# Six of eight u/gate pairs five tile pairs wide, eleven halves of their block sums by adding DMAs, every second pair with u first

## The chip, the cores and the metric

The kernel runs on one core of one Trainium2 chip. The metric is device time in microseconds for one execution. A core has a matrix engine (TensorE, PE in the profile, with its weight loads as PEld), a vector engine (VectorE, DVE), an activation engine (ScalarE, ACT), GpSimd (POOL) and a queue processor (SyncE, SP). DMAs are issued from the queues of SP, ACT and POOL and are carried out by the core's 16 DMA engines.

## The reference

Two decoder layers over a sequence of 256 rows with 2048 columns, then a norm. Only the first projection of the first layer matters here: `a_w_in` has 2048 rows and 3 x 4096 columns, u, v and gate.

```python
def gmlp_branch(xn, w_in, v_g, w_s, b_s, w_out):
    proj = xn @ w_in
    uv = jax.nn.gelu(proj[..., :2 * GMLP_WIDTH])
    zg = proj[..., 2 * GMLP_WIDTH:]
    u, v = jnp.split(uv, 2, axis=-1)
    v = rms_norm(v, v_g)
    ...
    mixed = jnp.einsum('gts,bnsgc->bntgc', ws, vc) + ...
    y = u * mixed * jax.nn.silu(zg)
    return y @ w_out
```

xn is 256 x 2048 here, w_in 2048 x 12288, and all data are float32.

## The kernel before, in words

**Products.** Every large product is a left side of 256 rows (two tiles of 128, t = 0 and 1) with a weight matrix. The weights come in k tiles of 128 rows and column blocks of 512. A tile is cut into a rounded high part (`cut`, line 114, on ACT) and the rest (line 115, on DVE), so that three matmuls (`terms`, lines 119 to 121: high by high, high by low, low by high) give a product of float32 accuracy. `cut` takes two tiles at a time, [128, 2, 512], or one, [128, 1, 512]; its results live in `wspl`, which has five buffers for each part.

**Pairs.** A `Pair` computes two column blocks j = 0 and 1 at once. For KS of its k tile pairs (one tile from each list of `HALVES`) it uses a scheme of seven block products instead of eight: with the left side's blocks a11 to a22 and the weights' blocks b11 (first list, column 0), b12 (first list, column 1), b21, b22 (second list), the products are called p1 to p7. The left side's sums S1 to S4 are made once (`Left.sums`, `Left.fifth`, `sums_of`). The weights' sums are made in place in b11 and b12. In the order of the code:

- `head`: p1 with b11 as it was loaded (bank a); then b11 becomes b12 - b11 (`minus`, line 286, DVE), and b12 gets b22 added (`plus`, line 294: a DMA issued by GpSimd that reads b22 from memory again and adds it); p5 with the new b11 (bank e); then b22 is added to b11 (line 314 on DVE for the first two groups, a DMA for the fifth tile).
- `body`: p6 with that b11 (bank b, begun from a copy of a); p2 with b21 (bank a); p7 with b12 (bank c, begun from a copy of b); then b11 becomes b21 - b11 (line 339, `minus`, DVE); p3 with b22 (bank b); p4 with the last b11 (bank d, begun from a copy of c).
- `column(0)` and `column(1)`: the k tiles outside the scheme, `rest`, two at a time, for both row tiles t; each step is 12 matmuls. Then `evac` takes the finished banks. `column(1)` of one pair runs in steps between the blocks of the next pair's head and body (`run`).

With 16 k tiles a pair has 7 x KS + 4 x (16 - 2 KS) = 64 - KS tile products of three matmuls.

**Groups and buffers.** `groups` cuts the KS tiles of a block into halves of two tiles and, when KS is 5, a fifth tile alone. With `fifth_first` the fifth comes first in p1 and p5 (`early`). Each half of b11, b12, b21 and b22 has one buffer in `sraw`, the fifth tiles of b11 and b12 have one each in `ex`, and the fifth tiles of b21 and b22 (`others`) and the tiles of `rest` share the three buffers of `wraw`.

**The stages.** v (columns of v, KS 4); gu (this case: eight pairs b = 0 to 7, column 0 the gate block, column 1 the u block, KS from `KS_GU`); o (the output product of the first layer); qk, bv and bg (the second layer); f (its output product). In gu, `mid_gu` between body and `column(0)` runs `mixing` for the pair: GpSimd loads `ws` behind the last adding DMA (line 596) and masks it (line 601), ACT and DVE cut it (lines 603 and 604), six matmuls mix (lines 616 to 618), ACT adds the bias (line 620). `evac_gu` applies silu to column 0 and gelu to column 1 on ACT (line 625) and multiplies y by it on DVE (at once for column 0, line 627; from a queue for column 1, line 532). When ACT goes from one of the two functions to the other it loads a table first (ACT_TABLE_LOAD at line 625).

**Order of work.** Each engine and each queue runs its own instructions in order. That order is fixed when the kernel is built, by a planner that simulates the engines' times and takes the work that is ready, mainly in the order of the code.

## Time and profile before

| | |
|---|---|
| median of 3 runs (lowest, highest) | 1143.83 us (1143.17, 1144.0) |
| profiled execution | 1143.73 us |
| its span, first to last instruction | 1142.0 us |
| mean granted TensorE clock | 0.998 |
| DMA packets | 264.72 MB, mean 232 GB/s |
| of it by GpSimd's queue (q0) | 33.04 MB, 15.7% of the 16 engines' span |
| of it by SP's queue (q1) | 227.57 MB, 56.9% |

How to read the lines: a row of groups gives source line, engine, operation, output<-inputs by the program's names, their shapes and the count, then the busy time in us and the mean ns of one, then the idle time of the engine just before them and what ended it. `gu_b` are the tiles of b11 to b22, `gu_p_hi` and `gu_p_lo` their cut parts, `gu_raw`, `gu_hi` and `gu_lo` the same for the columns, and `gu_a` to `gu_e` the banks (`gu_b` on TensorE is bank b). A row of windows gives the busy time of each engine in a stretch of the span, the granted clock, the DMA engines' mean busy share and GB/s. A row of the timeline gives start, length, engine, line and operation; neighbours of one kind are merged with a count.

### The profile page before, as it was taken

To read this page: it belongs to the slowest core of one execution; us is meant where nothing else is said; L and a number is where in the kernel's file an instruction comes from. 1 tells how busy PE (TensorE), PEld (TensorE's weight loads), DVE (VectorE), ACT (ScalarE), POOL (GpSimd) and SP (SyncE) were. 2 spreads that over 40 slices of the span, in tenths; PEclk is the share of its full clock that TensorE was granted. 3 is DMA by queue.
4 is the path that set the end of the run, shared out by engine and by line. 5 is a ranking of instruction groups with operands and counts; after the bars stand their busy time and mean duration, and the time that the engine had idled before them with its cause. 6 is when DMAs were issued, how large, how long until landed. Compare 5 with 4: busy or idle time off the path is not lost.

```text
span 1142.0 us, 14838 instructions
## 1 busy us (share of the span) xinstructions
PE 1132.6 (99%) x5168; PEld 939.5 (82%) x5168; DVE 1011.7 (89%) x1111; ACT 830.6 (73%) x1102; POOL 88.7 (8%) x106
## 2 busy tenths in 40 slices
PE   9999999999999999999999999999999999999997
PEld 6888888888888888888888888888888888888886
DVE  7989899988998999978988788989889989897986
ACT  8776777777787778866657456788678887886564
POOL 0300110100110110000010001100100101000000
PEclk9999999999999999999999999999999999999999
DMA  9978687686687786685785877687687766837962
GB/s 343 333 270 275 206 257 265 199 262 243 183 269 254 186 264 241 175 289 142 266 258 166 294 211 266 159 266 210 179 287 193 215 234 174 265 90 241 343 213 87
DMA packets 79083, 264.72 MB, mean 232 GB/s; under 512 B 8992, under 2 KB 9504, under 8 KB 78880
## 3 DMA queue, kind: packets, MB, share of 16 engines
q1 hardware_dynamic: 67040, 227.57, 56.9%
q0 software_dynamic: 10672, 33.04, 15.7%
q10 hardware_dynamic: 1296, 3.17, 0.7%
q8 instruction: 40, 0.66, 0.2%
q14 instruction: 35, 0.29, 0.1%
HBM read 259.55 MB, written 4.19 MB: 231 GB/s over the span
## 4 chain that ended last, share of the span: by engine, by line
PE 98%; ACT 0%; DMA 0%; issue 0%; SPq 0%; POOLq 0%; POOL 0%; DVE 0%; ACTq 0%
PE gu_a L121 3%; PE gu_a L120 3%; PE gu_b L121 3%; PE gu_b L120 3%; PE gu_a L119 3%; PE gu_b L119 3%; PE op_acc L119 2%; PE op_acc L121 2%; PE op_acc L120 2%; PE gu_d L121 2%; PE gu_c L121 2%; PE gu_d L119 2%; PE gu_d L120 2%; PE gu_c L120 2%; PE gu_c L119 2%; PE v_acc L120 1%
## 5 line engine op out<-in xcount | busy, mean ns | idle before, releaser
L114 ACT CAST gu_p_hi<-gu_b 128x1024 fp32r<-128x1024 f32 (+1 forms) x126 | 123.2, 1004 | 37.5 <-PE gu_c L121 17.5
L115 DVE TENSOR_TENSOR gu_p_lo<-gu_b,gu_p_hi 128x1024 fp32r<-128x1024 f32 (+1 forms) x126 | 143.1, 1166 | 2.9 <-ACT gu_p_hi L114 2.4
L115 DVE TENSOR_TENSOR qk_p_lo<-qk_b,qk_p_hi 128x1024 fp32r<-128x1024 f32 (+1 forms) x77 | 80.8, 1075 | 10.6 <-ACT qk_p_hi L114 10.1
L114 ACT CAST qk_p_hi<-qk_b 128x1024 fp32r<-128x1024 f32 (+1 forms) x77 | 70.5, 934 | 25.1 <-PE o_c L121 6.3
L115 DVE TENSOR_TENSOR gu_lo<-gu_raw,gu_hi 128x1024 fp32r<-128x1024 f32 x60 | 72.1, 1220 | 7.6 <-ACT gu_hi L114 7.3
L114 ACT CAST gu_hi<-gu_raw 128x1024 fp32r<-128x1024 f32 x60 | 61.9, 1052 | 18.9 <-DMA gu_raw<-in_a_w_in 7.9
L115 DVE TENSOR_TENSOR v_lo<-v_raw,v_hi 128x1024 fp32r<-128x1024 f32 (+1 forms) x41 | 48.9, 1195 | 13.5 <-ACT v_hi L114 13.4
L114 ACT CAST v_hi<-v_raw 128x1024 fp32r<-128x1024 f32 (+1 forms) x41 | 41.7, 1027 | 25.7 <-DMA v_raw<-in_a_w_in 20.2
L115 DVE TENSOR_TENSOR v_p_lo<-v_b,v_p_hi 128x1024 fp32r<-128x1024 f32 x42 | 50.4, 1221 | 4.8 <-ACT v_p_hi L114 4.6
L114 ACT CAST v_p_hi<-v_b 128x1024 fp32r<-128x1024 f32 x42 | 43.2, 1049 | 9.5 <-PE v_c L121 5.7
L115 DVE TENSOR_TENSOR bg_p_lo<-bg_b,bg_p_hi 128x1024 fp32r<-128x1024 f32 (+1 forms) x42 | 42.5, 1042 | 5.3 <-ACT bg_p_hi L114 5.3
L114 ACT CAST o_p_hi<-o_b 128x1024 fp32r<-128x1024 f32 (+1 forms) x35 | 33.4, 965 | 18.4 <-PE op_acc L121 13.4
L115 DVE TENSOR_TENSOR bv_p_lo<-bv_b,bv_p_hi 128x1024 fp32r<-128x1024 f32 (+1 forms) x42 | 42.5, 1041 | 4.4 <-ACT bv_p_hi L114 4.2
L114 ACT CAST bv_p_hi<-bv_b 128x1024 fp32r<-128x1024 f32 (+1 forms) x42 | 37.4, 907 | 10.0 <-PE qk_c L121 4.0
L114 ACT CAST bg_p_hi<-bg_b 128x1024 fp32r<-128x1024 f32 (+1 forms) x42 | 37.2, 907 | 8.9 <-PE bg_a L121 2.5
L115 DVE TENSOR_TENSOR o_p_lo<-o_b,o_p_hi 128x1024 fp32r<-128x1024 f32 (+1 forms) x35 | 38.3, 1113 | 5.4 <-ACT o_p_hi L114 5.4
L286 DVE TENSOR_TENSOR gu_b<-gu_b,gu_b 128x1024 f32<-128x1024 f32 (+1 forms) x36 | 41.3, 1164 | 0.1
L114 ACT CAST op_hi<-op_raw 128x1024 fp32r<-128x1024 f32 x24 | 25.0, 1052 | 19.0 <-PE op_acc L121 9.1
L114 ACT CAST o_hi<-o_raw 128x1024 fp32r<-128x1024 f32 x22 | 23.0, 1054 | 21.2 <-DMA o_raw<-in_a_w_out 12.1
L120 PE MATMUL op_acc<-op_lo,yc 128*128 128x512 f32 x96 | 37.8, 394 | 0.0
L115 DVE TENSOR_TENSOR o_lo<-o_raw,o_hi 128x1024 fp32r<-128x1024 f32 x22 | 26.7, 1224 | 12.3 <-ACT o_hi L114 12.0
L121 PE MATMUL op_acc<-op_hi,yc 128*128 128x512 f32 x96 | 37.6, 393 | 0.0
(798 smaller groups left out, 3775.8 us busy)
## 6 DMA issues: line engine op xcount, KB each, us to landing
gu_b<-in_a_w_in SPq DMA_DIRECT2D x64, 512.0 KB, 4.7
gu_raw<-in_a_w_in SPq DMA_DIRECT2D x60, 512.0 KB, 5.2
v_raw<-in_a_w_in SPq DMA_DIRECT2D x32, 512.0 KB, 5.2
qk_b<-in_b_w_in SPq DMA_DIRECT2D x32, 512.0 KB, 4.8
qk_raw<-in_b_w_in SPq DMA_DIRECT2D x26, 512.0 KB, 5.4
v_b<-in_a_w_in SPq DMA_DIRECT2D x24, 512.0 KB, 4.9
op_raw<-in_a_w_out SPq DMA_DIRECT2D x24, 512.0 KB, 4.5
o_raw<-in_a_w_out SPq DMA_DIRECT2D x22, 512.0 KB, 4.3
```

Source lines behind the costliest of these rows:

```text
L114: nc.scalar.copy(hi[:, sl], raw[:, sl])
L115: low[0] = nc.vector.tensor_sub(lo[:, sl], raw[:, sl], f(hi[:, sl]))
L119: nc.tensor.matmul(acc, lh, hi, start=first, stop=False, skip_group_check=True)
L120: nc.tensor.matmul(acc, lh, lo, start=False, stop=False, skip_group_check=True)
L121: nc.tensor.matmul(acc, ll, hi, start=False, stop=last, skip_group_check=True)
L286: nc.vector.tensor_sub(into[g], b0[g], b1[g])
```

## The change

Three settings change, and with them the signs of the sums.

- `KS_GU` goes from (4, 4, 4, 5, 4, 5, 4, 4) to (4, 5, 5, 5, 5, 5, 5, 4): pairs 1, 2, 4 and 6 become five tile pairs wide.
- A new list `FAR_GU` says for each pair how many of b11's two halves get b21 by an adding DMA, issued in the code right behind p6, in place of the DVE instruction ahead of p3: 0, 2, 2, 1, 2, 1, 2, 1, eleven halves in all. The fifth tile's sum stays on DVE.
- In every pair of odd number u is column 0 and the gate column 1, so that gelu ends one pair and begins the next, and then silu does.
- For a sum that a DMA can make, b21 must be added: so in the first two groups b11 is kept with its sign reversed (b11 - b12, then minus b22), S1 of the fifth tile and S2 of the others change sign to match, and the copy of bank e to `es` gets a scale of -1. This holds for the pairs of all stages.

```diff
-KS_GU = (4, 4, 4, 5, 4, 5, 4, 4)
+KS_GU = (4, 5, 5, 5, 5, 5, 5, 4)
+FAR_GU = (0, 2, 2, 1, 2, 1, 2, 1)
...
-        def minus(self, into, b0, b1, order=None):
-            for g in order or range(len(self.groups)):
-                nc.vector.tensor_sub(into[g], b0[g], b1[g])
-
-        def plus(self, into, i, j, g0=0):
+        def plus(self, into, i, j, g0=0, g1=9):
             for g in self.early:
-                if g < g0:
+                if not g0 <= g < g1:
                     continue
                 k, n = self.groups[g]
                 adds.append(nc.gpsimd.dma_start(into[g], self.src(HALVES[i][k], n, j), accum_op=ALU.add))
...
-            self.minus(self.b11, self.b12, self.b11, self.early)
+            for g in self.early:
+                b = (self.b11[g], self.b12[g])[::1 if g < 2 else -1]
+                nc.vector.tensor_sub(self.b11[g], *b)
...
             for g in range(len(self.b22)):
-                nc.vector.tensor_add(self.b11[g], self.b22[g], self.b11[g])
+                nc.vector.tensor_sub(self.b11[g], self.b11[g], self.b22[g])
...
-            nc.scalar.copy(es, e)
+            nc.scalar.activation(es, e, AF.Identity, scale=-1.0)
             block(b11, lambda k: left.sum_part(1, k), b, "p6")
+            self.plus(b11, 1, 0, 0, self.far)
...
-            self.minus(b11, b21, b11)
+            for g in range(self.far, len(self.groups)):
+                (nc.vector.tensor_add if g < 2 else nc.vector.tensor_sub)(b11[g], b21[g], b11[g])
...
-            nc.scalar.activation(sg, bank, (AF.Silu, AF.Gelu_apprx_tanh)[j], scale=r1[:, t:t + 1])
+            nc.scalar.activation(sg, bank, (AF.Silu, AF.Gelu_apprx_tanh)[(j + b) % 2], scale=r1[:, t:t + 1])
...
-            run(Pair(columns(a_w_in, 2 * W + b * CB, b * CB), left, KD, f"gu{b}", KS_GU[b],
-                     lambda j, t, bank, b=b: evac_gu(b, j, t, bank), mid=lambda pair, b=b: mid_gu(b, pair), fifth_first=True))
+            cs = 2 * W + b * CB, b * CB
+            run(Pair(columns(a_w_in, *cs[::-1 if b % 2 else 1]), left, KD, f"gu{b}", KS_GU[b],
+                     lambda j, t, bank, b=b: evac_gu(b, j, t, bank), mid=lambda pair, b=b: mid_gu(b, pair), fifth_first=True,
+                     far=FAR_GU[b]))
```

More of the change, by code (lines that the diff above doesn't have):

```diff
@@ L149, in sums @@
                 nc.vector.tensor_sub(s3, a21, a11)
-                nc.vector.tensor_sub(s2, a11, s1)
-                nc.vector.tensor_sub(s4, a12, s2)
+                nc.vector.tensor_sub(s2, s1, a11)
+                nc.vector.tensor_add(s4, a12, s2)
                 for i, si in enumerate((s1, s2, s3, s4)):
@@ L166, in fifth @@
             a11, a12, a21, a22 = full[:, 0, 0:P], full[:, 1, 0:P], full[:, 0, P:S], full[:, 1, P:S]
-            nc.vector.tensor_sub(sm[:, 0], a21, a22)
-            nc.vector.tensor_sub(sm[:, 1], a11, sm[:, 0])
+            nc.vector.tensor_sub(sm[:, 0], a22, a21)
+            nc.vector.tensor_add(sm[:, 1], a11, sm[:, 0])
             nc.vector.tensor_sub(sm[:, 2], a21, a11)
@@ L185, in sums_of @@
             nc.vector.tensor_sub(s13, a21, a22)
-            nc.vector.tensor_sub(s24, a11, s13)
+            nc.vector.tensor_sub(s24, s13, a11)
             split(0, s13)
@@ L189, in sums_of @@
             nc.vector.tensor_sub(s13, a21, a11)
-            nc.vector.tensor_sub(s24, a12, s24)
+            nc.vector.tensor_add(s24, a12, s24)
             split(2, s13)
@@ L233, in trunk_kernel, with __init__ @@
     class Pair:
-        def __init__(self, src, left, nk, name, ks, evac, mid=None, fifth=None, fifth_first=False):
+        def __init__(self, src, left, nk, name, ks, evac, mid=None, fifth=None, fifth_first=False,
+                     far=0):
             self.fifth = fifth or (lambda j, name: ex.tile([P, 1, CB], F32, tag=f"b1{j + 1}_2", name=name))
             self.src, self.left, self.name, self.ks = src, left, name, ks
-            self.evac, self.mid = evac, mid
+            self.evac, self.mid, self.far = evac, mid, far
             self.rest = [k for k in range(nk) if k not in HALVES[0][:ks] + HALVES[1][:ks]]
@@ L623, in evac_gu @@
             y = v_of(t, b * CB, CB)
-            sg = jk.tile([P, CB], F32, tag=f"sg{t}", bufs=1, name=f"{'gu'[j]}{b}_{t}")
-            nc.scalar.activation(sg, bank, (AF.Silu, AF.Gelu_apprx_tanh)[j], scale=r1[:, t:t + 1])
+            sg = jk.tile([P, CB], F32, tag=f"sg{t}", bufs=1, name=f"{'gu'[(j + b) % 2]}{b}_{t}")
+            nc.scalar.activation(sg, bank, (AF.Silu, AF.Gelu_apprx_tanh)[(j + b) % 2], scale=r1[:, t:t + 1])
             if j == 0:
```

## The prediction

> **What bounds the kernel now.** I read the chain of work that ended last first, then the stage that the change touches.
>
> ```profile
> PE 98%; ACT 0%; DMA 0%; issue 0%; SPq 0%; POOLq 0%; POOL 0%; DVE 0%; ACTq 0%
> ```
>
> The chain is TensorE almost from end to end: time is saved by giving it less to do, and lost where something else is late. The gu stage is the eight u/gate pairs. Below are the busy times from the mixing matmuls of pair 0 to those of pair 7, seven pair periods, with the first period alone above them, and one TensorE group of that window.
>
> ```profile
> core 0: us, PE busy (x) PEld busy (x) DVE busy (x) ACT busy (x) POOL busy (x), PEclk, DMA share, GB/s
> 194.61:236.77 42.16, 42.16 (x187) 34.92 (x186) 41.08 (x42) 31.98 (x37) 3.29 (x4) 1.00 0.75 233
> 194.61:488.50 293.89, 293.89 (x1300) 243.47 (x1299) 274.02 (x279) 226.51 (x270) 28.54 (x32) 1.00 0.74 230
> ```
>
> ```profile
> L121 PE MATMUL gu_a<-gu_p_hi,x_lo 128*128 128x512 f32 x60 | 23.4, 389 | 0.0
> ```
>
> TensorE is busy for all of the window, at clock 1.00, with 0.0 us of idle time before its instructions. A pair of width four has 3 x (7 x 4 + 4 x 8) = 180 matmuls and 6 for the mixing; 42.16 / 186 = 0.2267 us is what one matmul occupies (its mean of 389 ns is the pipelined duration). VectorE (DVE) is busy for 274.02 of 293.89 us, 93%, ScalarE (ACT) 77%, the DMA engines 74%: DVE is next in line.
>
> **Part 1, width five.** In general a pair has 3 x (64 - KS) matmuls. Pairs 1, 2, 4 and 6 go from four to five, 3 fewer each: 12 x 0.2267 = 2.72 us off TensorE. All of it is on the path if the others still deliver.
>
> What the others do for it, by the groups of the same window (DVE, then ACT):
>
> ```profile
> L115 DVE TENSOR_TENSOR gu_p_lo<-gu_b,gu_p_hi 128x1024 fp32r<-128x1024 f32 x98 | 117.8, 1225 | 2.5 <-ACT gu_p_hi L114 2.1
> L115 DVE TENSOR_TENSOR gu_lo<-gu_raw,gu_hi 128x1024 fp32r<-128x1024 f32 x54 | 64.9, 1219 | 3.2 <-ACT gu_hi L114 3.0
> L286 DVE TENSOR_TENSOR gu_b<-gu_b,gu_b 128x1024 f32<-128x1024 f32 x28 | 33.8, 1225 | 0.1
> ...
> L115 DVE TENSOR_TENSOR gu_p_lo<-gu_b,gu_p_hi 128x512 fp32r<-128x512 f32 x14 | 9.6, 683 | 0.0
> ...
> L286 DVE TENSOR_TENSOR gu_b<-gu_b,gu_b 128x512 f32<-128x512 f32 x4 | 2.7, 682 | 0.0
> ...
> L574 DVE TENSOR_TENSOR yc<-yT,yc 128x512 fp32r<-128x512 f32 x1 | 0.7, 690 | 0.2 <-ACT yc L573 0.2
> ```
>
> ```profile
> L114 ACT CAST gu_hi<-gu_raw 128x1024 fp32r<-128x1024 f32 x52 | 53.7, 1052 | 13.3 <-PE gu_d L121 6.6 <-DMA gu_raw<-in_a_w_in 2.3 <-DVE gu_lo L115 2.2
> L625 ACT ACT_TABLE_LOAD x14 | 18.0, 1283 | 0.2
> ...
> L114 ACT CAST gu_p_hi<-gu_b 128x512 fp32r<-128x512 f32 x14 | 8.7, 620 | 2.5 <-DMA gu_b<-in_a_w_in 0.8 <-PE gu_c L121 0.6 <-PE gu_b L121 0.5
> ...
> L328 ACT COPY gu_es<-gu_e 128x512 f32<-128x512 f32 x7 | 4.1, 588 | 2.1 <-PE gu_e L121 2.0
> ```
>
> A wider pair cuts seven half tiles more (one per block) and two full ones less (one per column), and makes two half sums more, for its first and third block sums. DVE: 4 x (7 x 0.683 - 2 x 1.219 + 2 x 0.682) = +14.8 us. ACT: 4 x (7 x 0.620 - 2 x 1.052) = +8.9 us.
>
> **Part 2, eleven sums by DMA.** Eleven of the L286 subtractions leave DVE: 11 x 1.225 = -13.5 us. DVE's fourteen groups (the first and the last are shown above) add to 288.8 us for 279 instructions where its busy time is 274.0, so each overlaps its neighbour by 0.05 us; the 17 instructions more in parts 1 and 2 give 0.9 back. Net for DVE +0.4 us: 274.4 of the new 291.2 us, 94% where it was 93%. On average it keeps up; where it is dense is rival B.
>
> In their place stand 11 adding DMAs on GpSimd's queue, and the wider pairs add two half-size ones each:
>
> ```profile
> L294 POOL DMA_DIRECT2D gu_b<-in_a_w_in x18 | 15.7, 870 | 207.3 <-DVE gu_b L286 137.7 <-DMA gu_raw<-in_a_w_in 55.1 <-ACT g L625 9.5
> L601 POOL TENSOR_SCALAR_AFFINE_SELECT ws<-ws 128x256 f32<-128x256 f32 x7 | 8.9, 1269 | 46.1 <-DMA ws<-in_wst 46.1
> ```
>
> ```profile
> q0 software_dynamic: 2928, 9.31, 17.5%
> ...
> gu_b<-in_a_w_in SPq DMA_DIRECT2D x8, 256.0 KB, 5.8
> ws<-in_wst POOLq DMA_DIRECT2D x7, 128.0 KB, 7.5
> ```
>
> ```profile
> DMA to landing us min/median/max: 4.1/6.9/8.6
> ```
>
> (The last row is GpSimd's adds.) Issue: 19 x 0.870 = 16.5 us on an engine busy for a tenth of the window. Does an add arrive in time? It has to wait until its half of b11 has been cut for p6, and p4's cut waits for it. The nearest case is pair 3, already five wide; the cuts of its second half and fifth tile for p6 on DVE, and of its second half for p4 on ACT:
>
> ```profile
> 302.05 2.03 DVE L115 TENSOR_TENSOR gu_p_lo<-gu_b,gu_p_hi 128x1024 fp32r<-128x1024 f32 x2
> ```
>
> ```profile
> 318.91 1.04 ACT L114 CAST gu_p_hi<-gu_b 128x1024 fp32r<-128x1024 f32 x1
> ```
>
> The second half is free at 304.1 at the latest, lands at 311.0 by the median and 312.7 by the longest landing, and is wanted at 318.9: 6 us to spare, so no cost. The first half is cut before it, but wanted only one cut earlier. Behind the adds on GpSimd's in-order queue wait the load of ws (it is ordered behind the last add) and its masking: issued at 305, landed at 312.5, masked for 1.27 us, ready at 314; ACT wants it here:
>
> ```profile
> 319.86 0.40 ACT L603 CAST wh<-ws 128x256 fp32r<-128x256 f32 x1
> ```
>
> Also 5 us to spare. The DMA engines do more: 11 x 0.524 + 8 x 0.262 = 7.86 MB of adds; plain loads stay at 32 tiles a pair (20 + 12 where there were 16 + 16). By the q0 row an added megabyte takes 0.175 x 293.89 / 9.31 = 5.52 us of all 16 engines, so +43 us: from 0.74 x 293.89 = 217 to 261 of 291.2 us, a share of 0.90. Whether this is on the path is rival C.
>
> The Trainium skill ("DMA: Bandwidth & Descriptors", Anatomy of one DMA — SWDGE) gives a DMA of this path 2.0 us plus its bytes at 436 GB/s. By that, an estimate, the 7.86 MB would take 18 us and the share come to 0.81, and a 512 KB add land in 3.2 us. The trace does not agree for adds that share the engines: 6.9 us to land and 5.5 us a megabyte. I go by the trace; by the page rival C would get half its chance.
>
> **Part 3, u first in every second pair.** Gelu then stands beside gelu and silu beside silu over the pair boundary; of 16 table loads 9 stay. ACT: -7 x 1.283 = -9.0 us, which cancels part 1's +8.9. ACT idles for 23% of the window, so neither is on the path. The multiplications stay as many.
>
> **Part 4, signs.** Every subtraction is replaced by one of the same form, in all stages. The copy of the e bank becomes an activation with a scale: between the 0.588 us of the copy and the 0.620 of a cast of that size, 0.03 us at most on an engine with slack; I take 0.
>
> **Sum.** The profiled execution took 1143.73 us (span 1142.0, 1.7 around it), 0.1 under the median of the runs. 1143.73 - 2.72 = **1141.0 us**, 0.24% less. A measurement of this kernel can tell about 0.2% (2.29 us) from no change, so the forecast clears it by only 0.4 us.
>
> **Rival B: the lead of DVE runs out in pairs 3 and 5.** TensorE starts on a tile after DVE has made its low part. In pair 3 of before the least lead is in p7:
>
> ```profile
> 313.97 1.23 DVE L115 TENSOR_TENSOR gu_p_lo<-gu_b,gu_p_hi 128x1024 fp32r<-128x1024 f32 x1 [0.22 <-ACT gu_p_hi L114]
> ```
>
> ```profile
> 316.10 0.39 PE L120 MATMUL gu_c<-gu_p_lo,xs 128*128 128x512 f32 x1
> ```
>
> Done at 315.20, used at 316.10: 0.9 us. In the changed kernel this pair has a column step less beside it: 12 matmuls (2.72 us) of cover go and one cut (1.17 after overlap) with them. One sum (1.17) goes too, so the lead is 0.9 - 2.72 + 1.17 + 1.17 = 0.5 us. With two sums by DMA it is 1.7. So pairs 1, 2, 4 and 6 are safe, and 3 and 5 just so. If the pair starts with one column step less of lead (1.55 us, since the pair ahead of it has a shorter column as well), 3 and 5 each stall for 1.0 us: 1143.0. For it: a margin of half a microsecond. Against it: the lead is refilled to the limit of the five cut buffers in each column. The place is p7 and p3; it decides from an entry lead 0.5 us lower. 1141.5 to 1143.0, chance 0.20.
>
> **Rival C, slower: the fifth tile of the next pair comes late.** In a wide pair p1 and p5 begin with the fifth tile. Its buffer is single and comes free after p4's last cut; before, no wide pair followed another, now it happens five times (1 to 2, up to 5 to 6). From pair 3, that last cut, and TensorE's first matmul of pair 4's p1:
>
> ```profile
> 321.79 0.69 DVE L115 TENSOR_TENSOR gu_p_lo<-gu_b,gu_p_hi 128x512 fp32r<-128x512 f32 x1
> ```
>
> ```profile
> 334.01 0.39 PE L119 MATMUL gu_a<-gu_p_hi,x_hi 128*128 128x512 f32 x1
> ```
>
> From 322.5 to 334.0 are 11.5 us for a landing of 5.8 and cuts of 0.62 + 0.68: 4.4 to spare. It turns critical from a landing of 10.2 us. It would be slower by over 0.2% if each of the five lost 1.0 us (5 less 2.7), a landing of 11.2; at 12.2 it is 1143.73 - 2.72 + 10 = 1151. For it: that load falls in the densest time of the DMA engines:
>
> ```profile
> 300.00:305.00 5.00, 5.00 (x24) 4.13 (x22) 5.00 (x5) 3.60 (x5) 0.70 (x1) 1.00 0.29 100
> 305.00:310.00 5.00, 5.00 (x24) 4.14 (x23) 5.00 (x7) 2.92 (x5) 0.00 (x0) 1.00 0.49 147
> ...
> 325.00:330.00 5.00, 5.00 (x24) 4.14 (x23) 4.49 (x5) 4.78 (x8) 0.28 (x1) 1.00 0.97 351
> ```
>
> Against it: the same rows show the adds of part 2, issued from 300 to 311, in the trough (0.29 and 0.49), not in the crowd. 1146 to 1151, chance 0.16.
>
> **Rival D: the instruction order moves elsewhere.** The order of each engine comes from a planner that simulates times; a shift of 2.7 us may reorder later stages.
>
> ```profile
> PE 1132.6 (99%) x5168; PEld 939.5 (82%) x5168; DVE 1011.7 (89%) x1111; ACT 830.6 (73%) x1102; POOL 88.7 (8%) x106
> ```
>
> Of TensorE's 9.4 us of idle time (1142.0 - 1132.6) a new order may win or add a tenth, about 1 us: 1140.0 to 1142.0, chance 0.11, of which 0.03 is clear of 0.2%.
>
> **How the numbers follow.** Forecast (1140.4 to 1141.4 by itself) 0.53, B 0.20, C 0.16, D 0.11. Faster: 0.53 + 0.03 = 0.56. Same: 0.20 + 0.08 = 0.28. Slower: C, 0.16. The range from 1140.2 to 1144.0 holds the forecast, B and nearly all of D, 0.83, and leaves out C.
>
> **What would show it.** Right: the gu stage shorter by 12 matmuls with TensorE's idle time there still 0.0; nine table loads; 21 full and 12 half subtractions for the block sums where the eight pairs had 32 and 4; the added DMAs landing in 7 to 9 us with nobody waiting for them; DMA share near 0.90. For B: TensorE idle before c or b matmuls of pairs 3 and 5, ended by DVE's L115. For C: TensorE idle at the start of pairs 2 to 6, behind an ACT cast that waits for a gu_b load from SP. The forecast is wrong if TensorE waits for over 0.4 us in all in this stage.

## The result

The changed kernel takes 1146.32 us (median of 9 runs, 1144.64 to 1148.16), the kernel before 1143.29 us beside it (9 runs, 1142.57 to 1144.18). The ratio is 1.0025 with an interval of [1.0016, 1.0033]: a quarter of a per cent slower, just beyond what can be told from no change. The forecast was 1141.0 in a range from 1140.2 to 1144.0, so sign and range were both wrong. The profiled execution of the changed kernel took 1144.64 us with a span of 1142.9; it is the fastest of the nine, so its trace shows the loss at its smallest.

### The profile page after: what moved, and what is told of

The parts are those of the page before. It is cut to its first block, busy times and chain, and to the rows that moved or that the text cites. A ratio compares the mean times of both kernels' runs of the same rounds, so it can differ in the third digit from the quotient of the medians.

```text
span 1142.9 us, 14923 instructions
## 1 busy us (share of the span) xinstructions
PE 1131.3 (99%) x5156; PEld 934.5 (82%) x5156; DVE 1012.0 (89%) x1128; ACT 826.9 (72%) x1115; POOL 110.6 (10%) x125
## 3 DMA queue, kind: packets, MB, share of 16 engines
q10 hardware_dynamic: 1296, 3.17, 0.7%
## 4 chain that ended last, share of the span: by engine, by line
PE 87%; DVE 5%; DMA 3%; issue 2%; ACT 2%; SPq 1%; POOLq 0%; POOL 0%; ACTq 0%; DVEq 0%
DVE gu_p_lo L116 2%; PE op_acc L122 2%; PE op_acc L121 2%; PE op_acc L120 2%; PE gu_b L121 2%; PE gu_b L122 2%; PE gu_b L120 2%; PE gu_a L121 2%; PE gu_a L122 2%; PE gu_a L120 2%; DMA gu_b<-in_a_w_in 2%; PE gu_c L121 1%; PE gu_c L122 1%; PE gu_c L120 1%; PE qk_a L122 1%
## 5 line engine op out<-in xcount | busy, mean ns | idle before, releaser
L115 ACT CAST gu_p_hi<-gu_b 128x1024 fp32r<-128x1024 f32 x154 | 137.6, 933 | 46.4 <-DVE gu_b L314 25.6
L116 DVE TENSOR_TENSOR gu_p_lo<-gu_b,gu_p_hi 128x1024 fp32r<-128x1024 f32 x154 | 160.3, 1079 | 5.6 <-ACT gu_p_hi L115 4.9
L116 DVE TENSOR_TENSOR qk_p_lo<-qk_b,qk_p_hi 128x1024 fp32r<-128x1024 f32 (+1 forms) x77 | 80.9, 1077 | 9.7 <-ACT qk_p_hi L115 9.2
L116 DVE TENSOR_TENSOR gu_lo<-gu_raw,gu_hi 128x1024 fp32r<-128x1024 f32 x52 | 62.8, 1222 | 16.5 <-ACT gu_hi L115 16.4
L115 ACT CAST gu_hi<-gu_raw 128x1024 fp32r<-128x1024 f32 x52 | 53.6, 1049 | 25.9 <-DMA gu_raw<-in_a_w_in 20.0
L116 DVE TENSOR_TENSOR v_lo<-v_raw,v_hi 128x1024 fp32r<-128x1024 f32 (+1 forms) x41 | 49.0, 1197 | 14.1 <-ACT v_hi L115 14.0
L292 POOL DMA_DIRECT2D gu_b<-in_a_w_in x39 | 33.7, 865 | 235.8 <-DVE gu_b L308 70.6
L116 DVE TENSOR_TENSOR v_p_lo<-v_b,v_p_hi 128x1024 fp32r<-128x1024 f32 x42 | 50.2, 1222 | 3.1 <-ACT v_p_hi L115 2.7
L116 DVE TENSOR_TENSOR bg_p_lo<-bg_b,bg_p_hi 128x1024 fp32r<-128x1024 f32 (+1 forms) x42 | 42.4, 1043 | 5.1 <-ACT bg_p_hi L115 5.1
L116 DVE TENSOR_TENSOR bv_p_lo<-bv_b,bv_p_hi 128x1024 fp32r<-128x1024 f32 (+1 forms) x42 | 42.5, 1042 | 5.0 <-ACT bv_p_hi L115 4.8
L115 ACT CAST o_p_hi<-o_b 128x1024 fp32r<-128x1024 f32 (+1 forms) x35 | 33.4, 965 | 18.4 <-PE op_acc L122 12.9
L115 ACT CAST bv_p_hi<-bv_b 128x1024 fp32r<-128x1024 f32 (+1 forms) x42 | 37.4, 908 | 10.2 <-PE qk_c L122 4.2
L116 DVE TENSOR_TENSOR o_p_lo<-o_b,o_p_hi 128x1024 fp32r<-128x1024 f32 (+1 forms) x35 | 38.3, 1115 | 5.4 <-ACT o_p_hi L115 5.4
L116 DVE TENSOR_TENSOR o_lo<-o_raw,o_hi 128x1024 fp32r<-128x1024 f32 x22 | 26.8, 1225 | 12.7 <-ACT o_hi L115 12.3
L122 PE MATMUL op_acc<-op_hi,yc 128*128 128x512 f32 x96 | 37.5, 393 | 0.0
```

Of the source, the lines that this page charges most:

```text
L115: nc.scalar.copy(hi[:, sl], raw[:, sl])
L116: low[0] = nc.vector.tensor_sub(lo[:, sl], raw[:, sl], f(hi[:, sl]))
L122: nc.tensor.matmul(acc, ll, hi, start=False, stop=last, skip_group_check=True)
L292: adds.append(nc.gpsimd.dma_start(into[g], self.src(HALVES[i][k], n, j), accum_op=ALU.add))
```

## The profile after

Most lines of the changed kernel's source have moved down by one to four: the cut's DVE part is L116, its three matmuls L120 to L122, loads L224, adding DMAs L292, the three kinds of block sums on DVE L308, L314 and L341.

First its chain of work that ended last (shares of the span), from its page:

```profile
PE 87%; DVE 5%; DMA 3%; issue 2%; ACT 2%; SPq 1%; POOLq 0%; POOL 0%; ACTq 0%; DVEq 0%
```

TensorE carried 98% of the chain before and carries 87% now. The rest is no longer hidden; where it lies shows below.

The gu stage between its first and its last mixing matmul, first before, then after (stretch; its length; busy time and count of PE, PEld, DVE, ACT, POOL; granted clock; DMA share; GB/s):

```profile
192.12:488.62 296.50, 296.50 (x1312) 245.61 (x1311) 276.63 (x282) 227.48 (x272) 28.54 (x32) 1.00 0.74 231
```

```profile
192.05:488.46 296.41, 295.83 (x1300) 242.56 (x1298) 275.66 (x298) 224.60 (x286) 50.30 (x51) 1.00 0.87 256
```

Twelve matmuls are gone, as forecast, but the stretch is only 0.09 us shorter where it should have been 2.72. DVE's busy time is as forecast as well (a shade less instead of +0.4). So TensorE waits for some 2.6 us. The row shows only 0.58 us of this as idle, because a matmul that waits can stand in the trace as a longer one (0.50 us in rows below, where the mean is 0.39); from here on "stalls" are therefore the distances between the starts of consecutive matmuls of the stage as far as they exceed 0.2267 us: 0.13 us before, 2.65 us after. After, 0.30 us of them are in pair 1, 0.35 in pair 3, 1.23 in pair 5 and 0.68 in pair 6. Who is waited for, from the waits of the stage (engine, line, what ended the wait; us in total, times, longest):

```profile
ACT gu_hi L115 <- DMA gu_raw<-in_a_w_in: 14.5, 5, 3.9
DVE gu_lo L116 <- ACT gu_hi L115: 12.8, 8, 2.3
...
ACT gu_p_hi L115 <- DMA gu_b<-in_a_w_in: 4.9, 7, 2.2
...
PEld gu_b L121 <- DVE gu_p_lo L116: 1.7, 4, 0.7
...
PEld gu_c L121 <- DVE gu_p_lo L116: 1.3, 3, 0.4
```

TensorE waits for DVE's cuts, in the banks b and c: in p6 and p7, and in steps of the pair before's column 1 that stand between them. DVE in turn waited for ACT, and ACT for loads. For loads of the columns ACT had waited 2.3 us in the whole stage before.

The chain in order of time shows what is late (start, length, what), here from the end of pair 3 to the cut of pair 4's first tile, and its like at the two boundaries that follow:

```profile
318.54 1.22 DVE gu_p_lo L116
319.77 0.32 DVE gu_c L344
320.28 0.76 DVE gu_p_lo L116
321.04 0.37 issue
321.41 0.44 DVE wl L606
321.95 0.45 SPq L224
322.49 6.29 DMA gu_b<-in_a_w_in
328.86 0.63 ACT gu_p_hi L115
329.51 0.70 DVE gu_p_lo L116
...
363.38 7.32 DMA gu_b<-in_a_w_in
...
391.87 0.50 PE gu_b L121
...
408.26 5.55 DMA gu_b<-in_a_w_in
```

When p4's last cut releases the single buffer, SP issues the load of the next pair's fifth tile (322.49); it lands 6 us later, ACT cuts it (328.86), DVE takes its low part, and from there on the chain is DVE's. TensorE does not stand still at this place. It stands still later, when what DVE has in hand is used up. Pair 4 gets through; the load for pair 5 goes out at 363.38 and takes 7.3 us, and in pair 5 the chain comes back to TensorE (391.87). There, in p6:

```profile
386.28 1.23 DVE L116 TENSOR_TENSOR gu_p_lo<-gu_b,gu_p_hi 128x1024 fp32r<-128x1024 f32 x1
```

```profile
387.56 0.50 PE L121 MATMUL gu_b<-gu_p_lo,xs 128*128 128x512 f32 x1 [0.18 <-DVE gu_p_lo L116]
```

The cut is done at 387.51 and used at 387.56. In pair 3, ahead of the boundary shown, the least lead was 0.9 us in p7 before; in the changed kernel:

```profile
313.94 2.96 DVE L116 TENSOR_TENSOR gu_p_lo<-gu_b,gu_p_hi 128x1024 fp32r<-128x1024 f32 x3
```

```profile
315.21 0.50 PE L121 MATMUL gu_c<-gu_p_lo,xs 128*128 128x512 f32 x1
```

The first of the three cuts is done at 313.94 + 1.22 = 315.16 and used at 315.21: TensorE has caught up with DVE.

The lead (from the end of DVE's low part to TensorE's first use of it) is short from the start of a pair on. At the start of p1 it was 5.2 us in pairs 3 and 5 before, and is 3.7 and 2.9 now; at the start of p6 it was 2.9 and 2.8, and is 0.6 and 0.1.

The other loss is at the very end. The program closes with a DRAIN on each engine, a sequencer instruction that the busy times do not count. The line on which it stands, before and after (engine, operation, count; shortest, median and longest in ns; first and last start):

```profile
L1196 POOLq DRAIN  x3: 46/93/5004, 1135.8 to 1141.8; - x3
L1196 SPq DRAIN  x3: 7/7/7, 1141.2 to 1141.5; - x3
```

```profile
L1200 POOLq DRAIN  x3: 46/93/6556, 1135.6 to 1142.6; - x3
L1200 SPq DRAIN  x3: 7/7/7, 1141.0 to 1142.4; - x3
```

Before, GpSimd's long DRAIN ran from 1135.8 to 1140.8, and SP, waiting for the output to land (1141.0), closed later, at 1141.2. After, it takes 6.56 us and ends at 1142.1, a whole microsecond behind SP. From the last matmul to the end it is 7.7 us before and 8.7 us after:

```profile
1134.35 0.39 PE L121 MATMUL f_c<-fl_hi,y_lo 128*128 128x512 f32 x1
```

```profile
1134.18 0.39 PE L122 MATMUL f_c<-fl_hi,y_lo 128*128 128x512 f32 x1
```

The difference of the two profiled executions: -2.72 (matmuls) + 2.52 (stalls) + 1.06 (closing) = +0.86 us; measured 1144.64 - 1143.73 = +0.91. The medians lie further apart; what the slower executions lose beside this is read from e5.

## The experiments

Each experiment's ratio is against the kernel before on the same chip (its medians there were between 1143.73 and 1144.00); that of "after" is against the 1143.29 above. "Tail" is the time from the last matmul to the end.

| run | edit | median us | ratio [95%] | stalls us | GpSimd DMAs, DRAIN us | tail us |
|---|---|---|---|---|---|---|
| before | | 1143.83 | | 0.13 | 83, 5.00 | 7.68 |
| after | | 1146.32 | 1.0025 [1.0016, 1.0033] | 2.65 | 102, 6.56 | 8.74 |
| e1 | width alone | 1153.23 | 1.0087 [1.0074, 1.0101] | 11.9 | 91, 5.66 | 7.84 |
| e2 | adds alone | 1144.20 | 1.0008 [0.9999, 1.0017] | 0.21 | 94, 5.90 | 8.24 |
| e3 | u first alone | 1143.31 | 0.9998 [0.9989, 1.0006] | 0.12 | 83, 5.00 | 7.67 |
| e4 | before + 19 small DMAs | 1143.56 | 1.0000 [0.9991, 1.0009] | as before | 102, 6.19 | 8.38 |
| e5 | after, again | 1146.62 | 1.0022 [1.0013, 1.0030] | 4.77 | 102, 6.56 | 8.74 |
| e6 | fifth tile last | 1144.22 | 1.0001 [0.9993, 1.0010] | 0.32 | 102, 6.56 | 8.74 |
| e7 | b21's and b22's fifth tiles in own buffers | 1149.47 | 1.0048 [1.0036, 1.0060] | 6.88 | 102, 6.56 | 8.74 |
| e8 | e6 and e7 | 1143.17 | 0.9993 [0.9985, 1.0002] | 0.21 | 102, 6.56 | 8.75 |
| e9 | wide pairs apart | 1143.47 | 0.9996 [0.9987, 1.0005] | 1.12 | 98, 6.23 | 8.42 |
| e10 | two fifth buffers | 1143.95 | 1.0000 [0.9991, 1.0008] | 1.84 | 102, 6.56 | 8.74 |
| e11 | after, 17 loads from ACT | 1145.85 | 1.0020 [1.0012, 1.0029] | 2.84 | 85, 5.46 | 7.64 |
| e12 | e8, 17 loads from ACT | 1144.09 | 1.0002 [0.9993, 1.0011] | 0.37 | 85, 5.46 | 7.65 |
| e13 | after, 13 later loads from ACT | 1145.32 | 1.0013 [1.0004, 1.0022] | 3.80 | 89, 5.70 | 7.89 |
| e14 | e8, loads kept in order | 1143.22 | 0.9996 [0.9988, 1.0005] | 0.91 | 102, 6.56 | 8.74 |
| e15 | e14, 14 later loads from ACT | 1142.63 | 0.9989 [0.9981, 0.9998] | 1.82 | 88, 5.66 | 7.85 |
| e16 | e15, pair 1 on shared buffers | 1141.39 | 0.9978 [0.9969, 0.9987] | 0.21 | 88, 5.66 | 7.85 |
| e17 | e16, pair 1 without far adds | 1141.72 | 0.9984 [0.9975, 0.9992] | 0.58 | 86, 5.49 | 7.78 |

Stalls, DRAIN and tail are those of one profiled execution, the median is that of 3 to 11 runs; the profiled execution can be a fast or a slow one of these.

### One part at a time

e1 is the kernel before with one line of the change.

```diff
-KS_GU = (4, 4, 4, 5, 4, 5, 4, 4)
+KS_GU = (4, 5, 5, 5, 5, 5, 5, 4)
```

> The kernel before with KS_GU of the kernel after, and nothing else of the change. Theory (the pairs lose their lead: VectorE idles at each pair boundary for tiles that load late, and has no lead left for the dense stretch from p5 to p3; beside it GpSimd's closing drain grows with the number of its DMAs): without the eleven adds VectorE needs 274.0 + 14.8 - 28 x 0.05 = 287.4 us of 291.2 in the window of seven pair periods, and its idle time there (20 us in both kernels) does not fit into the 4 us that are left, so TensorE stalls for 10 us or more: 1143.3 - 2.7 + 10 to 16 = 1150 to 1157. Rival (the traffic of the adding DMAs is what makes everything late): without it the forecast of 2.7 us less holds, 1140.6 to 1141.5.

e2 is the changed kernel with the widths and the column order of before, so that the eleven adds (and the signs) are left.

```diff
-KS_GU = (4, 5, 5, 5, 5, 5, 5, 4)
+KS_GU = (4, 4, 4, 5, 4, 5, 4, 4)
...
-            run(Pair(columns(a_w_in, *cs[::-1 if b % 2 else 1]), left, KD, f"gu{b}", KS_GU[b],
+            run(Pair(columns(a_w_in, *cs), left, KD, f"gu{b}", KS_GU[b],
```

> The kernel after with KS_GU of the kernel before and the gate first in every pair: only the eleven sums by DMA. Theory: no wide pair follows another, VectorE has 13.5 us less to do, so the gu stage is as long as before with no stall; GpSimd has 11 DMAs more, its closing drain goes from 5.0 to 5.9 us, 0.4 of it on the path: 1143.3 to 1143.9. Rival (traffic of the adds): the DMA share rises from 0.74 to about 0.85, loads land late and TensorE stalls in the stage for 1 us or more: 1145 or more.

e3 is the changed kernel with the widths of before and no added DMAs; u first in every second pair and the signs are left.

```diff
-KS_GU = (4, 5, 5, 5, 5, 5, 5, 4)
-FAR_GU = (0, 2, 2, 1, 2, 1, 2, 1)
+KS_GU = (4, 4, 4, 5, 4, 5, 4, 4)
+FAR_GU = (0,) * 8
```

> The kernel after with KS_GU of the kernel before and no sums by DMA: only u first in the odd pairs, and the signs. Theory: nine table loads in place of sixteen, ScalarE 9 us less busy, TensorE as before: 1143.1 to 1143.6. Rival (the new order of the work by itself costs time): 1144.5 or more, with idle time of TensorE in the stage.

The width alone costs 9.4 us in the median instead of saving 2.7, in the stage and through stalls. Its profiled execution, the slowest of four, took 11.4 us more than that of the kernel before: -2.72 + 11.8 (stalls) + 0.2 (tail) + 1.7 (first u/gate matmul at 162.8 instead of 161.1) = 11.0. The stage of e1, first to last mixing matmul:

```profile
193.81:500.24 306.43, 301.33 (x1302) 241.63 (x1300) 288.75 (x309) 231.73 (x292) 34.52 (x40) 1.00 0.74 229
```

The DMA engines are no busier than before (0.74), which rules out traffic as the cause here. DVE is busy for 94% of this stretch, and TensorE waits in every pair from 1 to 6. The same 288.75 us are 98% of the 293.8 that TensorE needs for its matmuls, so how much of e1's loss is DVE's load and how much the order of its work, this run alone does not tell. The adds take 12 us off DVE (e2: 264.90 us busy, share of the DMA engines 0.84) with 0.21 us of stalls: at the widths of before they neither disturb the stage by their traffic nor arrive late. (e2's median is 0.3 us above its range; its longer tail is explained below.) What they do in the changed kernel is to repair most of what the width breaks, 11.9 us of stalls down to 2.65. The order of u and gate and the signs do nothing that can be measured.

### The spread of the changed kernel

e5 is the changed kernel once more, unaltered.

> The kernel after once more, beside the variants of it, for a second profile: the first profiled execution was the fastest of nine (1144.64, median 1146.3). Theory (lead lost at the pair boundaries): TensorE's stalls in the gu stage, 2.6 us in the first profile, are 3 to 6 us in one that takes the median time, in the same places (p5 to p3 of pairs 1 to 6), and the time is 1145.5 to 1147. Rival (the longer times come from outside the stage): stalls of 2.6 us as before and the rest elsewhere.

The profiled execution took 1147.56 us, 2.9 more than the first. Its tail is the same to the hundredth; the stalls are 4.77 us instead of 2.65, and its first u/gate matmul came 0.6 us later. The runs of the changed kernel spread over 3.5 and 4.3 us, those of the kernel before beside them over 1.6 (9 runs) and 2.6 us (29 runs). A lead near zero, which turns a difference in a landing into time, would explain this; it is not shown.

### The fifth tile at the boundary

e6 alters one word: in p1 and p5 the fifth tile comes last.

```diff
-                     lambda j, t, bank, b=b: evac_gu(b, j, t, bank), mid=lambda pair, b=b: mid_gu(b, pair), fifth_first=True,
+                     lambda j, t, bank, b=b: evac_gu(b, j, t, bank), mid=lambda pair, b=b: mid_gu(b, pair), fifth_first=False,
```

> The kernel after with the fifth tile behind the two halves in p1 and p5 of the gu pairs (fifth_first off): the tile whose single buffer comes free last is wanted last. Theory: the wait for the fifth tile goes, the wait for the third step of column 0 stays (19.8 us of ScalarE's time in the kernel after, 12.8 of VectorE's), so less than half of the stalls go: 1144.5 to 1146. Rival (traffic of the adds): no change, 1146 to 1146.7. Rival (only the fifth tile matters): all stalls go, 1143.3 - 2.7 + 1.0 for the drain = 1141.6.

e7 leaves the order and gives the fifth tiles of b21 and b22 buffers of their own instead of two of `wraw`'s three (paid for by `pb`, one buffer instead of two).

```diff
-                raw = wraw.tile([P, 2, CB], F32, tag="raw", name=f"{self.name}_b1{j}_{g}")
+                raw = (ex.tile([P, 1, CB], F32, tag=f"b2{j + 1}_2", name=f"{self.name}_b1{j}_{g}") if self.name[0] == "g"
+                   else wraw.tile([P, 2, CB], F32, tag="raw", name=f"{self.name}_b1{j}_{g}"))
...
-        pb = lg.enter_context(tc.tile_pool(name="pb", bufs=2))
+        pb = lg.enter_context(tc.tile_pool(name="pb", bufs=1))
```

> The kernel after with buffers of their own for the fifth tiles of b21 and b22 in the gu pairs, so that the three buffers of the columns' tiles are not shared with them (to make room the mixing's small tiles get one buffer where they had two). Theory: ScalarE no longer waits for the third step of column 0, but the fifth tile of the next b11 still comes late, right behind it: 1144.5 to 1146. Rival (traffic): no change, 1146 to 1146.7. Rival (only the columns' buffers matter): 1141.6.

e8 has both edits.

> Both of the two edits before together. Theory: neither wait is left at the boundary, VectorE enters each wide pair with a lead of 4 us or more, TensorE's stalls in the stage fall under 0.7 us; what stays is the longer closing drain (1.0 us): 1143.3 - 2.7 + 1.0 + 0.5 = 1141.6 to 1142.4. Rival (traffic of the adds): stalls of 2 us or more stay, 1144.5 to 1146.7.

e9 is the changed kernel with four wide pairs, none behind another.

```diff
-KS_GU = (4, 5, 5, 5, 5, 5, 5, 4)
+KS_GU = (4, 5, 4, 5, 4, 5, 4, 5)
```

> The changed kernel with its wide pairs apart: KS 4, 5, 4, 5, 4, 5, 4, 5 in place of 4, 5, 5, 5, 5, 5, 5, 4, nothing else altered. Four wide pairs where the kernel before has two, no wide pair behind another, six matmuls fewer than before (1.36 us). GpSimd's DMAs are 98, so its closing drain is about 6.3 us, 0.8 us beyond SP's. Theory (the lead goes at the boundary between two wide pairs, where the fifth tile, wanted first, has its one buffer free last): the stage's stalls are under 0.6 us, and the time is 1143.3 - 1.36 + 0.3 + 0.8 = 1143.0, from 1142.4 to 1143.6. Rival (the lead goes in any wide pair, since its column is a step shorter and the DMA engines are fuller): stalls of 1.5 us or more in pairs 1, 3, 5 and 7, and 1144.0 or more.

e10 leaves the fifth tile first and gives those of b11 and b12 a second buffer.

```diff
-        ex = lg.enter_context(tc.tile_pool(name="exg", bufs=1))
-        pb = lg.enter_context(tc.tile_pool(name="pb", bufs=2))
+        ex = lg.enter_context(tc.tile_pool(name="exg", bufs=2))
+        pb = lg.enter_context(tc.tile_pool(name="pb", bufs=1))
```

> The changed kernel with two buffers in place of one for the fifth tiles of b11 and b12 in this stage (paid for by one buffer less for the mixing's ws, wm, wh and wl), the fifth tile still first in p1 and p5. Theory A (the single buffer is what makes the fifth tile late): it can be loaded a pair ahead, the stalls fall under 0.7 us, and the time is 1144 to 1144.8, as when the fifth tile comes last. Theory B (the place of the fifth tile in the order, whatever its buffer: a half tile first gives TensorE 2.7 us of work less to stand on before the first full tile is wanted): the stalls stay at 1.5 us or more and the time at 1145.5 or above.

One word removes the stalls of the profiled execution, more than the theory asked for: it took 1142.10 us, its stage 293.81 us, which is 1296 matmuls (seven pairs, mixing included) by 0.2267 to within a hundredth:

```profile
191.98:485.79 293.81, 293.81 (x1299) 243.07 (x1297) 276.08 (x298) 226.33 (x285) 46.67 (x51) 1.00 0.87 259
```

DVE's load is not what differs: it is busy for 276.08 us here and 275.66 in the changed kernel. But this execution is the second fastest of eleven, the median is 2.1 us above it, and the runs spread over 4.2 us, so the others may still lose something. The lead at the start of p6 is 2.7 and 2.3 us in pairs 3 and 5 of this trace.

How it works shows in ACT's timeline at the boundary from pair 3 to pair 4, first in the changed kernel, then in e6 (start, length, line, operation, idle before and what ended it):

```profile
319.92 2.00 ACT L115 CAST gu_hi<-gu_raw 128x1024 fp32r<-128x1024 f32 x2
325.02 1.05 ACT L115 CAST gu_hi<-gu_raw 128x1024 fp32r<-128x1024 f32 x1 [3.10 <-DMA gu_raw<-in_a_w_in]
...
328.86 2.53 ACT L115 CAST gu_p_hi<-gu_b 128x512 fp32r<-128x512 f32 x3 [0.41 <-DMA gu_b<-in_a_w_in]
```

```profile
319.12 2.01 ACT L115 CAST gu_hi<-gu_raw 128x1024 fp32r<-128x1024 f32 x2
323.91 1.05 ACT L115 CAST gu_hi<-gu_raw 128x1024 fp32r<-128x1024 f32 x1 [2.79 <-PE gu_a L120]
325.18 1.06 ACT L115 CAST gu_p_hi<-gu_b 128x1024 fp32r<-128x1024 f32 x1 [0.22 <-DMA gu_b<-in_a_w_in]
```

After the same two column cuts ACT cuts the next pair's first tile 8.9 us later in the changed kernel and 6.1 us later in e6, and there it is a full half, not a half-size tile. ACT runs in order: while the fifth tile, loaded last, is the first to be cut, the two halves, loaded before it, wait behind it. ACT's own idle time at this place is much the same in both (3.10 + 0.41 and 2.79 + 0.22 us); by which steps the later cut becomes a shorter lead in p6 and p7 was not followed through.

The second buffer of e10 reaches nearly the same time (1143.95) with the order unaltered, though 1.84 us of stalls are left in its profile, where the theory that it is the buffer asked for less than 0.7 and the theory that it is the order for 1145.5. Without stalls the changed kernel would take about 1142.2 us (1143.83 - 2.72 + 1.06), so either remedy takes about half of the loss away in the medians: the order and the single buffer both have a part. e9 points the same way: pairs 3, 5 and 7, wide behind a narrow one, do not stall at all, though the narrow pairs between them also give DVE less to do (271.77 us of its stage's 301.51). All its 1.12 us are in pair 1, which the theory had not foreseen (more on it below).

The loads of the columns seem to have a part too. ACT waited for them for 2.3 us in the kernel before and 14.5 in the changed one (pairs 0 to 6); it is 18.4 us in e10, 7.7 in e6 and 0.3 in e8. e8, with 0.21 us of stalls, is 1.05 us below e6 in the median, inside both intervals, and its runs lie within 1.5 us. It is 0.8 us above its own range all the same; 0.7 of this is a later start, told below.

e7 was a miss: it was to help a little, and cost 3 us with 6.88 us of stalls. ACT's wait for column loads is down to 1.8 us there, so that wait is not the cause by itself: it does not help to end it while the fifth tile is late. Why the edit does harm was not settled.

### The closing DRAIN

e4 is the kernel before with 19 small DMAs more on GpSimd, in the o stage, where nobody waits for them. They load data that is not used.

```diff
+    dmy = const.tile([P, 19], F32, name="dmy")
+    with tc.issue_after(ins_of(adds[-1])):
+        for i in range(19):
+            nc.gpsimd.dma_start(dmy[:, i:i + 1], gcols[:, i:i + 1])
```

> The kernel before with 19 small DMAs more on GpSimd's queue in the o stage ([128, 1] each, read by nobody). Theory: the closing drain of GpSimd takes as long as in the kernel after, 6.6 us where it was 5.0, and ends 1.0 us after SyncE's: span and time 1.0 us longer, 1144.3, with TensorE's last matmul where it was. Rival (the drain goes by the bytes or by the adding of the late adds, not by the number of DMAs): drain 5.0 us, 1143.3.

e11 is the changed kernel with the loads of `ws`, `vg` and `gf` issued from ScalarE's queue; e12 is e8 with the same edit.

```diff
-            nc.gpsimd.dma_start(vg, a_v_norm_g[0:1, b * CB:(b + 1) * CB].to_broadcast([P, CB]))
+            nc.scalar.dma_start(vg, a_v_norm_g[0:1, b * CB:(b + 1) * CB].to_broadcast([P, CB]))
...
-                nc.gpsimd.dma_start(ws, wst[:, b * GPB:(b + 1) * GPB, :])
+                nc.scalar.dma_start(ws, wst[:, b * GPB:(b + 1) * GPB, :])
```

> The changed kernel with 17 of GpSimd's loads (ws, vg, gf) issued from ScalarE's queue, nothing else altered. GpSimd has 85 DMAs instead of 102, so by the drain theory its closing drain is about 5.2 us and ends within 0.3 us of SP's: 1.0 us off the end, with the stalls of the gu stage as in the changed kernel (2.6 to 4.8 us): 1145.4, from 1144.8 to 1146.0. Rival (the drain is hidden by the end of the execution, as the small DMAs in the kernel before hinted): the drain row shrinks and the time stays within 0.4 us of the changed kernel's 1146.4.

> The version with the fifth tile last and buffers of their own for the columns' fifth tiles, and 17 of GpSimd's loads issued from ScalarE's queue. Both theories' repairs together: stalls in the gu stage under 0.6 us, a drain of about 5.2 us that ends with SP's. If the drain is on the path, 1143.17 - 1.0 = 1142.2, from 1141.7 to 1142.7; if it is not, 1143.0 to 1143.4. What the prediction asked for would be 1143.3 - 2.7 = 1140.6.

`gf` is moved the same way. e13 moves only those whose buffer is still in use when they come up.

```diff
-            nc.gpsimd.dma_start(vg, a_v_norm_g[0:1, b * CB:(b + 1) * CB].to_broadcast([P, CB]))
+            (nc.scalar if b > 1 else nc.gpsimd).dma_start(vg, a_v_norm_g[0:1, b * CB:(b + 1) * CB].to_broadcast([P, CB]))
...
-                nc.gpsimd.dma_start(ws, wst[:, b * GPB:(b + 1) * GPB, :])
+                (nc.scalar if b >= 2 else nc.gpsimd).dma_start(ws, wst[:, b * GPB:(b + 1) * GPB, :])
```

> The changed kernel with 13 of GpSimd's loads issued from ScalarE's queue: only those whose buffer is in use when they come up (ws from pair 2 on, vg from block 2 on, gf), so that none can slip to the start of the kernel, as vg and ws did in the run before (issued at 1.3 and 5.2 us, and the first u/gate matmul 3.4 us later). 89 DMAs on GpSimd: a drain of about 5.7 us. If the drain is on the path, the time from the last matmul to the end falls by 0.8 us against the changed kernel's and the median to about 1145.6; if it is hidden, the median stays within 0.3 us of 1146.4. The gu stage's stalls stay between 2 and 5 us under both.

The DRAIN goes by the number of GpSimd's DMAs and not by their bytes: 5.00, 5.66, 5.90, 6.23 and 6.56 us with 83, 91, 94, 98 and 102, which is 0.082 us for each add, whether of 512 KB (e2) or 256 KB (e1), and 1.19 us more for the 19 small ones of e4, 0.063 each. A load moved away takes 0.064 to 0.066 us off it (e11, e13, e15). The tail follows: 7.7 us in the kernel before and in e3, where the DRAIN ends ahead of SP, 8.7 in the seven executions where it ends 1.05 us behind it, 7.9 in e13:

```profile
L1200 POOLq DRAIN  x3: 46/102/5698, 1137.7 to 1143.9; - x3
L1200 SPq DRAIN  x3: 7/7/7, 1143.3 to 1143.6; - x3
```

(e2's 8.24 is another thing: there GpSimd is done ahead of SP, and the output itself landed half a microsecond later.) In the medians the evidence is weaker. e13 is 1.0 and 1.3 us below the two medians of the changed kernel, as expected, but the intervals overlap. And e4, whose profile shows a tail 0.7 us longer, is no slower in the median than the kernel before: a miss that stays open, though its interval of about 1 us either way does not rule out 0.7. So the microsecond is shown in the profiled executions and not in the medians. e11 and e12 changed more than was meant: the moved loads of `vg` and `ws` were issued at 1.3 and 5 to 6 us, in competition with the first weights, and the first u/gate matmul came at 164.4 and 163.6 us instead of 161.1. Their tails (7.64, 7.65) say what e13's does.

### Both repairs

e14 is e8 with one word more. In e8 the new buffers were free from the start, two of their loads slipped to 5.5 and 8.3 us after the start, and the first u/gate matmul came 0.7 us late; now each is kept behind the load before it.

```diff
-                load(raw[:, 0:n], self.src(HALVES[1][k], n, j))
+                load(raw[:, 0:n], self.src(HALVES[1][k], n, j), behind=True)
```

> The version with the fifth tile last and buffers of their own for the columns' fifth tiles, with those loads kept behind the load before them in SP's order; in the earlier run the first two slipped to 5.5 us after the start and the first u/gate matmul came 0.8 us later. The boundary theory: stalls in the gu stage under 0.6 us, the first u/gate matmul at 161.0, the time before's 1143.9 - 2.7 + 1.06 (drain) = 1142.3, from 1141.8 to 1142.8. Rival (the width's saving is taken elsewhere): 1143.2 as before the repair.

e15 is e14 with the edit of e13 (`ws` from pair 1 on).

> The same with 14 of GpSimd's loads (ws from pair 1 on, vg from block 2 on, gf) on ScalarE's queue. 88 DMAs on GpSimd, a drain of about 5.7 us that ends 0.2 us after SP's. Stalls under 0.6 us. If boundary and drain are the whole loss, the prediction's 2.7 us come back: 1143.9 - 2.7 + 0.2 = 1141.4, from 1141.0 to 1142.0. If something else of the change costs time, 1142.5 or more.

e16 takes the own buffers away from pair 1.

```diff
-                raw = (ex.tile([P, 1, CB], F32, tag=f"b2{j + 1}_2", name=f"{self.name}_b1{j}_{g}") if self.name[0] == "g"
+                raw = (ex.tile([P, 1, CB], F32, tag=f"b2{j + 1}_2", name=f"{self.name}_b1{j}_{g}") if self.name[0] == "g" and self.name != "gu1"
```

> Both repairs, but pair 1 (behind the narrow pair 0) takes its columns' fifth tiles from the shared buffers again, as in the changed kernel. With buffers of their own they were issued at 210.0 and 210.6 us, together with pair 1's adding DMAs, landed after 10 us, and pair 1 stalled for 1.6 us. If that crowd is what is left of the loss: stalls under 0.6 us in the stage and 1141.2 to 1142.0. If pair 1's adds alone make the crowd, its stalls stay above 0.7 us and the time at 1142.6.

e17 is e16 with FAR_GU (0, 0, 2, 1, 2, 1, 2, 1).

> The same, and pair 1's two sums with b21 back on VectorE (FAR_GU 0 instead of 2 for pair 1). Two adding DMAs less in pair 1, 2.3 us more on VectorE there. If the adds crowd out the loads of pair 1, it gains on the run beside it (by up to 1 us); if VectorE's lead is short in pair 1, it loses; by the prediction's working (pair 1 has 1.7 us of lead with its two sums by DMA, so less than nothing without them) it stalls for over 0.6 us in p7 and p3 of pair 1.

e14 and e15 were above their ranges: pair 1 stalls there by 0.70 and 1.60 us. The loads that no longer slipped to the start are now issued at 208 and 210 us, among pair 1's adds. What comes late is one of these adds, that of b22 to the fifth tile of b11, which p6 needs. In e15 it is issued at 215.72 and lands at 223.03; ACT waits for it, and the column cut behind it in ACT's order is what TensorE then waits for:

```profile
223.13 0.62 ACT L115 CAST gu_p_hi<-gu_b 128x512 fp32r<-128x512 f32 x1 [3.53 <-DMA gu_b<-in_a_w_in]
```

```profile
225.24 0.50 PE L120 MATMUL gu_b<-gu_hi,x_hi 128*128 128x512 f32 x1 [0.69 <-ACT gu_hi L115]
```

ACT waits at the same cut of pair 1 for 2.18 us in the changed kernel, 3.23 in e9 and 3.75 in e14. In e16 the add lands after 4.9 us instead of 7.3, and the stalls are gone. The chain is TensorE's again:

```profile
PE 98%; ACT 0%; DMA 0%; issue 0%; SPq 0%; POOLq 0%; POOL 0%; DVE 0%; ACTq 0%
```

```profile
192.34:486.01 293.67, 293.67 (x1298) 243.23 (x1297) 276.80 (x298) 227.69 (x285) 39.49 (x44) 1.00 0.90 259
```

No idle time, the stage 2.83 us shorter than before, and 1141.39 us against 1143.83 of the kernel before: ratio 0.9978 [0.9969, 0.9987]. The sum, 1143.83 - 2.72 + 0.08 (stalls) + 0.17 (tail) = 1141.4, closes. e16 is the fastest version of the study, and it has all six wide pairs and all eleven adds. e17 stalls for 0.37 us in pair 1 and is 0.3 us behind e16, inside both intervals; the 0.6 us expected from the prediction's working were too many.

## Why the prediction was wrong

**Right.** The price of a matmul and their number; DVE's load in the stage (275.66 us where 276.63 were, "+0.4" forecast); the nine table loads; that ACT's saving and the signs are worth nothing (e3); that the sums by DMA cost the stage nothing at the widths of before (e2). The sums came out as counted, 21 full and 12 half ones besides the 16 with b22, which are L314:

```profile
L308 DVE TENSOR_TENSOR gu_b<-gu_b,gu_b 128x1024 f32<-128x1024 f32 x16 | 19.5, 1221 | 0.0
...
L341 DVE TENSOR_TENSOR gu_b<-gu_b,gu_b 128x1024 f32<-128x1024 f32 x5 | 6.3, 1261 | 0.0
...
L308 DVE TENSOR_TENSOR gu_b<-gu_b,gu_b 128x512 f32<-128x512 f32 x6 | 4.1, 689 | 0.1
L341 DVE TENSOR_TENSOR gu_b<-gu_b,gu_b 128x512 f32<-128x512 f32 x6 | 4.1, 686 | 0.0
```

The DMA share went to 0.87 and the adds land after 6.5 us by the median:

```profile
gu_b<-in_a_w_in POOLq DMA_DIRECT2D x25, 512.0 KB, 6.5
```

The forecast from the rows was 0.90 and 7 to 9 us. An estimate by the Trainium skill ("DMA: Bandwidth & Descriptors", Anatomy of one DMA — SWDGE) gave 0.81 and 3.2 us. The share came out between the two, and for the landing the rows of before were by far the better guide. The share did not decide the case.

**The first step that failed: "the lead is refilled to the limit of the five cut buffers in each column."** This was the argument against rival B, and it holds only where the next pair's first tile is there to be cut when the column runs out of cuts. Behind a wide pair it is not. The prediction had seen the lateness itself (rival C: the single buffer, free after p4's last cut, 4.4 us to spare), but it measured the slack from the landing to TensorE's first use, found it positive, and closed the account. C's stall at the start of a pair indeed never came: the landings shown took 5.6 to 7.3 us, where it asked for over 10.2. That C's range, 1146 to 1151, holds the measured median is luck. What the slack did not count is what ACT and DVE could have done in the meantime: both run in order, the fifth tile is first in their order, and the microseconds by which the halves are cut later come out of the lead that p6 and p7 of this and the next pairs live on. That the order and the buffer of this tile decide is shown (e6, e10); this way from the one to the other is argued. So C's place feeds B's mechanism: B's own condition, an entry lead at least 0.5 us lower, was met with 1.5 and 2.3 us in pairs 3 and 5; the two rivals were priced as alternatives, each with a margin of its own, and their sum was not. B was looked for in pairs 3 and 5 alone, and 1, 2, 4 and 6 were called safe. Without the adds it is in all six (e1), with them in 1, 3, 5 and 6 of the first profile and in 2 to 6 of e5's.

**The second: Part 2 took the 19 GpSimd DMAs at the cost of their issue.** "Issue: 19 x 0.870 = 16.5 us on an engine busy for a tenth of the window" is right, and they left a debt that falls due outside the window: the closing DRAIN grew by 1.56 us, of which 0.5 was hidden before SP's end and 1.06 stood on the tail of the profiled execution. The trace of before showed the row (5.00 us, ended 0.5 us ahead of SP), on the line of the program's end; the prediction did not look there, because it is in no list of busy times. Part 2's question whether an add arrives in time was also put to the sums with b21 in pair 3 alone, with 6 us to spare. The half-size adds of the wide pairs have no such margin: ACT waited 0.76 us for pair 3's before, and 2.18 for pair 1's after.

**The size.** With both mended the prediction's own sum holds: 1141.0 was forecast, 1141.39 measured in e16. The term of 2.72 us was true, the zero beside it was not. The 1.06 us of the closing DRAIN in it rest on the profiled executions.

**Open.** Why own buffers with the fifth tile first are worse (e7); why e4's longer tail is not in its median; and what makes the add of pair 1's fifth tile late in e9, e14 and e15: that the stall went when two loads left the place (e16) is shown, that taking out two adds instead would have done it as well was not tried.

## What to carry to other kernels

When an engine runs in order ahead of the bottleneck, a late tile costs what that engine could have done in the meantime, not only what the bottleneck waits for: take it from the smallest lead downstream, and add up rivals that can happen together. The tile whose buffer comes free last should stand last in the order. Before adding DMAs to GpSimd, look at its closing DRAIN and at what else ends the program.

## What the runs showed of the hardware

- GpSimd's DRAIN at the end of the program grows with the DMAs that it has issued in the whole program, however long ago they landed: from 5.00 us with 83 to 6.56 us with 102, 0.082 us for each add of 256 or 512 KB and 0.063 us for each DMA of 512 bytes (e4).
- Adds and loads bring the DMA engines to a share of 0.90 in the stage (e16) with no idle time of TensorE and 0.21 us of stalls; a share of 0.90 is no bound by itself here.
- A matmul that waits can show as a longer matmul: 2.65 us of stalls in the stage stood as 0.58 us of idle time in its row, and single matmuls took 0.50 us where the mean is 0.39. The distances between starts tell it.
